# A hybrid diffusion layer: the prompt's output projection and feed-forward moved in between the sample's scan units

## The chip, the cores and the metric

The kernel runs on one core of a Trainium2 chip, as one program. The metric is the device time in microseconds (us), the median of several runs. Engines: PE is TensorE (matrix products), PEld its weight loads, DVE is VectorE, ACT is ScalarE, POOL is GpSimd, SP is SyncE, which issues most transfers here. Every engine works its own queue strictly in order; where two engines depend on each other, one waits at a semaphore.

## The reference

One layer, run for two groups of tokens that share all weights: a prompt of 256 tokens and a sample of 1024 tokens (a grid of 16 rows and 64 columns). The model width is 1024, the feed-forward width 2816, everything is float32. Cut to what matters:

```
h = rmsnorm(x, g_norm1) * (1 + scale_m) + shift_m
proj = h @ w_in
hc, gb, gc, z, xbc, dtf, dtb = split(proj)
out_a = gb * dwconv1d(gc * hc, w_conv_short)
xs, bm, cm = split(silu(dwconv1d(xbc, ...)))
y = ssd_scan(forward) + ssd_scan(backward) + xs * d_skip      # chunks of 128 tokens
y = rmsnorm(y * silu(z), g_ssd_norm)
x = x + gate_m * (concatenate([out_a, y]) @ w_out)
h2 = rmsnorm(x, g_norm2) * (1 + scale_f) + shift_f
u = h2 @ w_up
u = dwconv2d_grid(u) if sample else dwconv1d(u)
ug, uv = split(u)
x = x + gate_f * ((silu(ug) * uv) @ w_down)
y_out = rmsnorm(x, g_final)
```

The modulation vectors (shift, scale, gate) come from a conditioning vector through `w_ada`. The prompt and the sample never mix: the prompt's scan starts from zero, the sample's from given states, and the prompt's final states are outputs.

## The kernel before

Activations lie with channels on the 128 partitions and tokens along the free axis, in eight blocks `k` of 128 channels. A float32 product is made of three: each operand is split in a high part (rounded to the matmul type) and a low part, and `mm3` (line 142) issues, for each `k`, high x high (147), high x low (149) and low x high (151). A weight tile of 1024 x 128 numbers (512 KB) goes through `wload` (line 132): SP loads it into `raw` (line 135), ACT copies it to `whi` (137), and POOL or DVE subtracts to `wlo` (line 73, a helper that records every two-operand operation). `raw` has two buffers, `whi` and `wlo` three each. While the norm pool is open, the prompt's projections pass a buffer of their own to `wload`, from the tag `x` with eight buffers, instead of `raw`.

The stages, by the time at which they lie on the trace: norm statistics, conditioning and first projections (0 to 75 us); the prompt's projections, 24 weight tiles against 256 columns (75 to 162); the sample's scan inputs (162 to 259); the scan (259 to 520); the join of gate, output projection of the first tokens and their norm (520 to 630); the feed-forward (630 to 1618).

The scan has a first pass for both groups and then a second pass of units: 4 for the prompt, 16 for the sample, one unit for each chunk and each of two groups of heads. For a unit, `prep` (lines 559 to 580) loads the decay sums broadcast over partitions into `csb` (562, two buffers), adds a mask on DVE (73), takes eight exponentials on ACT (570) and one of `csb` (572); two units later `output` (line 592) multiplies on PE. `prep` of unit i + 2 is written behind `output` of unit i. Between the units stand *fillers*: the sample's remaining projections, one weight tile against twice 512 columns, 48 matmuls each. `fill` gives one to every second prompt unit and to two of three sample units; what is left runs behind the scan.

Then the gate (lines 695 to 722) multiplies y by silu(z), normalizes and splits it, and the output projection and the feed-forward run in two blocks of tokens: block A, 704 tokens (the prompt's 256 and 448 of the sample), and block B, 576 of the sample. So a weight tile of `w_out` (763) or `w_up` (833) is loaded once for each block and feeds 256 + 448 or 256 + 320 columns, as pairs of matmuls. The feed-forward walks six groups of 4, 4, 4, 4, 3 and 3 channel blocks: up tiles of gate and value, convolution taps on DVE (76, a helper), silu, product and split, and the down projection of the group before (903). A block's edge row for the grid convolution goes through DRAM, as does block B's normalized input.

The order within each engine's queue is set by a scheduler that places the program's instructions by their dependencies and its own estimates.

Of the kernel before, what the change touches and what calls it, by code (L numbers as in the profile page):

```python
# [26 lines left out]
TA = TP + 7 * GW  # L27
TB = TT - TA
OA = TP + 6 * GW
OB = TT - OA  # L30
# [23 lines left out]
def body(nc, tc, A):  # L54
# [6 lines left out]
    def open_pool(name, side="left", **kw):  # L61
        g = tc.tile_pool(name=name, bufs=1, side=side, **kw)
        return g, g.__enter__()
# [50 lines left out]

    g_hs, hsp = open_pool("hsp", side="right")
    g_cv, cv = open_pool("cv", side="right")
    g_xy, xy = open_pool("xy", side="right")
# [24 lines left out]
    def mm3(outs, wh, wl, n):  # L142

        mms = []
        for k in range(n):
            for o, rh, rl in outs:
                nc.tensor.matmul(o, wh[:, k, :], rh(k), start=k == 0, stop=False)  # L147
            for o, rh, rl in outs:
                nc.tensor.matmul(o, wh[:, k, :], rl(k), start=False, stop=False)  # L149
            for o, rh, rl in outs:  # L150
                mm = nc.tensor.matmul(o, wl[:, k, :], rh(k), start=False, stop=k == n - 1)  # L151
# [102 lines left out]
    def ada_block(k):  # L254
        wa = [T(xy, [P, 4, 2 * P], "xs", 4) for _ in range(2)]
        for i in range(2):
            dma(wa[i], A["w_ad1"][k, i])
        pm = psa()
        for j in range(KT):
            q = 32 * (j % 4)  # L260
            nc.tensor.matmul(pm[q:q + 32, 0:2 * P], sc[:, j, :], wa[j // 4][:, j % 4, :],
# [70 lines left out]
    oad = T(dr, [4, 2, P, TT], "oad", 1)  # L332
    zd = T(dr, [4, P, TT], "zd", 1)
# [38 lines left out]
    def zproj(s, j, lo_eng):  # L372
        pp = proj(s, 12 + j, lo_eng)
        z = T(cv, [P, s.T], "xl", 2)
        act(z, pp, AF.Copy)
        nc.scalar.dma_start(zd[j, :, s.t0:s.t0 + s.T], z)
# [105 lines left out]
    def tok_major(s, c, want_raw, r0):  # L482
# [10 lines left out]
        xd = T(sw[0], [P, 512], "xd", 4)  # L493
# [3 lines left out]
        if want_raw:  # L497
            xtok = T(sw[0], [P, 512], "xd", 4)
            act(xtok, xt, AF.Copy)
# [34 lines left out]
    def ssd_pass2(s, fill):  # L534
# [69 lines left out]
        for i in range(2 * s.nc):  # L604
            output(*us[i], fill(s, i))
# [19 lines left out]
    SS.X = [T(xy, [P, TS], "xs", 4) for _ in range(4)]  # L625
# [10 lines left out]
    silu = act(bcall, bcall, AF.Silu)  # L636
    for j in range(4):
# [8 lines left out]
    dts = dtstage(SS, d4_s, silu)  # L646
# [4 lines left out]
    for i in range(N_LOOP, 8):  # L651
# [3 lines left out]
        if i >= 4:  # L655
            ada(i - 2, lambda: T(nrm, [P, 1024], "x", 8))
# [3 lines left out]
    mask = sm[:, wff0:wff0 + 2 * L].rearrange("p (a l) -> p a l", a=2)  # L660
    dma(mask, A["cst"][:, 168:168 + 256].rearrange("p (a l) -> p a l", a=2))
    SP.mask = SS.mask = mask

    def fillers():
        for j in range(4):
            zproj(SS, j, PG)
            yield
        for j in range(4):
            yield from outa(SS, j, PG)

    filler = fillers()

    def fill(s, i):

        if i % 2 == 0 if s.name == "p" else i % 3 != 2:
            next(filler, None)
            return mid_mm[0]
# [442 lines left out]
```

## Time and profile before

| what | us |
| --- | --- |
| median of 3 runs | 1621.23 (1620.62 to 1623.91) |
| the profiled execution's own time | 1629.9 |
| its span | 1628.1 |
| PE busy | 1548.7 |
| DVE busy | 1095.6 |
| ACT busy | 646.3 |
| POOL busy | 519.1 |
| read from / written to device memory | 167.89 MB / 23.67 MB |

Busy times are sums over the span; engines overlap. Matmuls are pipelined, so a matmul's duration on the trace is longer than the spacing of two in a row, and the spacing is what counts for time. PEclk is the share of TensorE's full clock that was granted. In lists of waits each line tells which engine and line waited, for whom, us in total, times, and the longest. A list of one tile gives min/median/max in ns, the first and last start, and the shapes.

### The profile page before, as it was taken

The page shows a single profiled execution, that of the slowest core. Times are in us where ns is not written, and L with a number is a line of the kernel's source. Part 1 is how long each engine was busy: PE and PEld are TensorE (multiplying, and loading weights), DVE is VectorE, ACT ScalarE, POOL GpSimd, SP SyncE. Part 2 cuts the span into 40 slices and gives each one's busy share as a digit, 9 for nine tenths or more (in the row PEclk, how much of TensorE's full clock was granted, in tenths as well). Part 3 has the DMA queues.
Part 4 walks back from the last instruction along what each step waited for, and adds up shares of the span by engine and source line. Part 5 has one row for each costly group of instructions (what it writes and reads, how often), then busy time and mean ns, then how long its engine had stood idle before and what let it go on. Part 6 is the DMA issues. An engine that isn't in the chain of part 4 may idle for free. (4 is left out here: it accounts for less than half of the span.)

```text
span 1628.1 us, 24939 instructions
## 1 busy us (share of the span) xinstructions
PE 1548.7 (95%) x9942; PEld 1411.9 (87%) x9942; DVE 1095.6 (67%) x1637; ACT 646.3 (40%) x1005; POOL 519.1 (32%) x288
## 2 busy tenths in 40 slices
PE   6989999888899799999999999999999999999997
PEld 2688767677777689999999999999999999999996
DVE  5664625445555636698666697656798777887685
ACT  6553534344445424343333353323334232433233
POOL 0445010011111000234434443434455444444442
PEclk8999999999999899999999999999999999999998
DMA  8555275534333551422222243222622223332221
GB/s 295 208 182 162 73 255 191 155 99 78 105 115 128 198 197 53 131 73 86 65 85 79 70 156 115 77 70 70 200 94 92 89 82 98 125 114 73 84 62 65
DMA packets 99534, 193.19 MB, mean 119 GB/s; under 512 B 9274, under 2 KB 51786, under 8 KB 99418
## 3 DMA queue, kind: packets, MB, share of 16 engines
q1 hardware_dynamic: 97690, 188.46, 35.9%
q10 hardware_dynamic: 1728, 3.15, 0.5%
q8 instruction: 78, 1.28, 0.3%
q14 instruction: 38, 0.31, 0.1%
HBM read 167.89 MB, written 23.67 MB: 118 GB/s over the span
## 5 line engine op out<-in xcount | busy, mean ns | idle before, releaser
L76 DVE SCALAR_TENSOR_TENSOR cc<-acc,sm,cc 128x384 f32<-128x384 f32 (+7 forms) x836 | 547.1, 665 | 114.8 <-ACT cc L855 44.9
L73 POOL TENSOR_TENSOR wlo<-raw,whi 128x1024 fp32r<-128x1024 f32 (+2 forms) x115 | 271.6, 2362 | 848.2 <-ACT whi L137 707.7
L137 ACT ACTIVATE whi<-raw 128x1024 fp32r<-128x1024 f32 x126 | 133.1, 1057 | 319.0 <-PE acc L149 279.6
L147 PE MATMUL acc<-ya,whi 128*128 128x256 f32 (+2 forms) x768 | 178.8, 315 | 10.7 <-ACT yb L718 7.7
L149 PE MATMUL acc<-ya,whi 128*128 128x256 f32 (+2 forms) x768 | 178.6, 314 | 0.0
L151 PE MATMUL acc<-ya,wlo 128*128 128x256 f32 (+2 forms) x768 | 177.7, 313 | 0.0
L149 PE MATMUL acc<-oa,whi 128*128 128x256 f32 (+2 forms) x768 | 176.3, 311 | 0.0
L151 PE MATMUL acc<-oa,wlo 128*128 128x256 f32 (+2 forms) x768 | 175.9, 311 | 0.0
L147 PE MATMUL acc<-oa,whi 128*128 128x256 f32 (+2 forms) x768 | 175.8, 311 | 0.0
L76 DVE SCALAR_TENSOR_TENSOR x<-dn,mod,x 128x320 f32<-128x320 f32 (+2 forms) x176 | 96.1, 546 | 91.8 <-PE dn L151 91.1
L147 PEld LDWEIGHTS acc<-ya,whi 128*128 128x128 f32 x768 | 138.8, 191 | 14.0 <-ACT yb L718 8.1
L149 PEld LDWEIGHTS acc<-ya,whi 128*128 128x128 f32 x768 | 139.5, 191 | 3.5 <-issue 0.2
L151 PEld LDWEIGHTS acc<-ya,wlo 128*128 128x128 f32 x768 | 139.1, 191 | 3.4 <-issue 0.2
L151 PEld LDWEIGHTS acc<-oa,wlo 128*128 128x128 f32 x768 | 137.6, 189 | 3.0
L147 PEld LDWEIGHTS acc<-oa,whi 128*128 128x128 f32 x768 | 137.5, 189 | 3.0
L149 PEld LDWEIGHTS acc<-oa,whi 128*128 128x128 f32 x768 | 137.5, 189 | 3.0
L73 POOL TENSOR_TENSOR dlo<-draw,dhi 128x512 fp32r<-128x512 f32 (+1 forms) x88 | 107.7, 1225 | 78.1 <-ACT dhi L912 78.1
L147 PE MATMUL acc<-h,whi 128*128 128x512 f32 x352 | 113.7, 404 | 3.8 <-DVE xs L76 3.8
L149 PE MATMUL acc<-h,whi 128*128 128x512 f32 x352 | 112.7, 399 | 0.0
L151 PE MATMUL acc<-h,wlo 128*128 128x512 f32 x352 | 112.4, 398 | 0.0
L147 PE MATMUL dn<-yb,dhi 128*128 128x320 f32 (+2 forms) x352 | 108.9, 309 | 1.8 <-DVE x L76 1.8
L151 PE MATMUL dn<-yb,dlo 128*128 128x320 f32 (+2 forms) x352 | 108.7, 309 | 0.0
(283 smaller groups left out, 3030.2 us busy)
## 6 DMA issues: line engine op xcount, KB each, us to landing
raw<-in_w_up SPq DMA_DIRECT2D x88, 512.0 KB, 3.5
x<-in_w_ada SPq DMA_DIRECT2D x32, 512.0 KB, 7.4
draw<-in_w_down SPq DMA_DIRECT2D x64, 256.0 KB, 2.8
x<-in_w_in SPq DMA_DIRECT2D x24, 512.0 KB, 4.0
raw<-in_w_in SPq DMA_DIRECT2D x22, 512.0 KB, 4.5
xs<-in_w_ad SPq DMA_DIRECT2D x16, 512.0 KB, 5.1
csb<-csds SPq DMA_DIRECT2D x16, 512.0 KB, 9.1
raw<-in_w_out SPq DMA_DIRECT2D x16, 512.0 KB, 3.6
```

The source lines that it names most:

```text
L73: (eng or V).tensor_tensor(out=out, in0=a, in1=b, op=op)
L76: V.scalar_tensor_tensor(out=out, in0=a, scalar=s, in1=b, op0=op0, op1=op1)
L137: act(hi, raw, AF.Copy)
L147: nc.tensor.matmul(o, wh[:, k, :], rh(k), start=k == 0, stop=False)
L149: nc.tensor.matmul(o, wh[:, k, :], rl(k), start=False, stop=False)
L151: mm = nc.tensor.matmul(o, wl[:, k, :], rh(k), start=False, stop=k == n - 1)
```

## The change

The prompt's tokens are taken out of the two token blocks. The scan is reordered: first both passes of the prompt's scan, with a filler in each of its four units, then the prompt's gate; then the sample's first pass with a filler at every second step; then the sample's 16 units. Units 0 to 7 have one filler each. At unit 8 the pools of the normalized inputs are closed, and a generator `prompt_steps` starts: eight output projection tiles for the prompt's 256 tokens, statistics and second norm, 44 up tiles, 24 down tiles (two blocks of 128 outputs in one `raw` tile) and the final norm. It has 54 steps of one or two weight tiles each; five are taken in each of the last eight units, and the rest behind the scan. All of it goes through `raw`. Each of those units also gates a chunk of 128 tokens (`gate_chunk`) and stores it to DRAM.

The sample's output projection and feed-forward then run in two blocks of 512 tokens, one matmul of 512 columns for each product; the feed-forward's second block starts 64 tokens earlier for the grid's edge row, so that the down projection has 448 and 576 tokens. The second block's normalized input stays on chip. z gets its silu when it is projected, and SP instead of ACT stores it. Four conditioning loads move: two into the prompt's projections, two within the sample's. The output projection runs its k in the order 4 to 7, 0 to 3. Counted over the program: 8736 products before and 7488 now, with the same columns; weight loads of `w_up` rise from 88 to 132, of `w_out` from 16 to 24, and 56 half tiles of `w_down` are added; POOL instructions rise from 284 to 372, DVE's from 1628 to 1685.

```diff
...
-    def mm3(outs, wh, wl, n):
+    def mm3(outs, wh, wl, ks):
 
         mms = []
-        for k in range(n):
+        ks = list(range(ks)) if isinstance(ks, int) else ks
+        for k in ks:
             for o, rh, rl in outs:
-                nc.tensor.matmul(o, wh[:, k, :], rh(k), start=k == 0, stop=False)
+                nc.tensor.matmul(o, wh[:, k, :], rh(k), start=k == ks[0], stop=False)
             for o, rh, rl in outs:
                 nc.tensor.matmul(o, wh[:, k, :], rl(k), start=False, stop=False)
             for o, rh, rl in outs:
-                mm = nc.tensor.matmul(o, wl[:, k, :], rh(k), start=False, stop=k == n - 1)
+                mm = nc.tensor.matmul(o, wl[:, k, :], rh(k), start=False, stop=k == ks[-1])
...
-        act(z, pp, AF.Copy)
-        nc.scalar.dma_start(zd[j, :, s.t0:s.t0 + s.T], z)
+        s.zact = act(z, pp, AF.Silu)
+        dma(zd[j, :, s.t0:s.t0 + s.T], z)
...
+        if j in (1, 3):
+            ada_s(2 + j // 2)
...
-            ada(i - 2, lambda: T(nrm, [P, 1024], "x", 8))
+        if i in (3, 5):
+            ada_s(4 + i // 5)
...
+    for step in ssd_pass1(SP):
+        step()
+    ssd_pass2(SP, lambda i: project())
...
+    steps = ssd_pass1(SS)
+    for i, step in enumerate(steps):
+        step()
+        if i % 2 == 1:
+            project()
+        if i == 1:
+            gate_p()
+
+
+    ph = Norm()
+
+    def open_prompt():
+        close_pool(g_hs)
+        close_pool(g_cv)
+        ph.g_mx, ph.mx = open_pool("mx", side="right")
+        ph.g_pf, ph.pf = open_pool("pf", side="right")
...
+    def prompt_steps():
+        pf = ph.pf
+        mix = load_mix(ph.mx, 0, TP)
+        x1 = [T(pf, [P, 4, TP], "x1p", 2) for _ in range(2)]
+        for q in range(2):
+            dma(x1[q], xT[:, 4 * q:4 * q + 4, 0:TP])
+        xv = [x1[m // 4][:, m % 4] for m in range(KT)]
...
+        for m in range(KT):
+            if m % 2 == 0:
+                pps = pair_psum()
+            wh, wl = split_wout(m)
+            pp = pps[m % 2]
+            last_mm.append(mm3([(pp, lambda k: mix[k][0], lambda k: mix[k][1])], wh, wl, KS)[-1])
+            stt(xv[m], pp, col(2, m, 0), xv[m], ALU.mult, ALU.add)
             yield
...
+        def up(m, pp, out, lo_eng):
+            wh, wl = wload(A["w_up"][m], lo_eng)
+            last_mm.append(mm3([(pp, lambda k: h2[k][:, 0], lambda k: h2[k][:, 1])], wh, wl, KT)[-1])
+            w = [smv("wff")[:, m * 9 + t:m * 9 + t + 1] for t in range(9)]
+            act(out, pp, AF.Identity, scale=w[4], bias=smv("bff")[:, m:m + 1])
...
+        def down(gi, g, m):
+            nj = GROUPS[gi]
+            j0 = sum(GROUPS[:gi])
+            raw = T(wst, [P, KT, P], "raw", 2)
+            for i in range(2):
+                off = (j0 * KT + (m + i) * nj) * P * P
+                dma(raw[:, i * nj:(i + 1) * nj],
+                    A["w_down"][off:off + nj * P * P].rearrange("(p j c) -> p j c", p=P, j=nj))
+            wh = T(wst, [P, KT, P], "whi", 3, F32R)
+            act(wh[:, 0:2 * nj], raw[:, 0:2 * nj], AF.Copy)
+            wl = T(wst, [P, KT, P], "wlo", 3, F32R)
+            tt(wl[:, 0:2 * nj], raw[:, 0:2 * nj], wh[:, 0:2 * nj].bitcast(F32), ALU.subtract, PG)
+            pps = pair_psum()
+            for i in range(2):
+                mm = mm3([(pps[i], lambda k: g[0][:, k], lambda k: g[1][:, k])],
+                         wh[:, i * nj:(i + 1) * nj], wl[:, i * nj:(i + 1) * nj], nj)
+                last_mm.append(mm[-1])
+                stt(xv[m + i], pps[i], col(5, m + i, 0), xv[m + i], ALU.mult, ALU.add)
...
+            for i in range(nj):
+                pps = pair_psum()
+                up(j0 + i, pps[0], cg[:, i], PG)
+                up(N_FF + j0 + i, pps[1], cu[:, i], PV if i % 2 else PG)
+                yield
+                if prev is not None:
+                    down(gi - 1, prev, 2 * i)
+                    if i == nj - 1 and nj < 4:
+                        down(gi - 1, prev, 6)
+                    yield
...
+        for m in range(0, KT, 2):
+            down(len(GROUPS) - 1, prev, m)
+            yield
...
+    def gate_chunk(c):
...
+        hi = T(pf, [P, 4, L], "gh", 1, F32R)
+        act(hi, uf, AF.Copy)
+        tt(u, uf, hi.bitcast(F32), ALU.subtract)
+        for i, src in enumerate((hi, u)):
+            dma(yd[:, i, :, tl].rearrange("j p t -> p j t"), src.bitcast(F32))
...
-    def fill(s, i):
-
-        if i % 2 == 0 if s.name == "p" else i % 3 != 2:
-            next(filler, None)
-            return mid_mm[0]
...
+    N_PROJ = 8
+    more = [None]
+
+    def fill_s(i):
+        if i < N_PROJ:
+            return project()
+        if i == N_PROJ:
+            for _ in filler:
+                pass
+            open_prompt()
+            more[0] = prompt_steps()
+        else:
+            gate_chunk(i - N_PROJ - 1)
+        for _ in range(N_FILL):
+            next(more[0], None)
         return last_mm[-1]
 
-    for step in ssd_pass1(SS) + ssd_pass1(SP):
-        step()
-    ssd_pass2(SP, fill)
-    ssd_pass2(SS, fill)
-    for _ in filler:
-        pass
+    N_FILL = 5
+    ssd_pass2(SS, fill_s)
+    gate_chunk(7)
...
+    for _ in more[0]:
+        pass
...
+    def wout(mix, a):
         for m in range(KT):
+            wh, wl = split_wout(m)
+            pp = pac()
+            mm3([(pp, lambda k: mix[k][0], lambda k: mix[k][1])], wh, wl, KS)
+            xx = x1[m][:, a:a + HB]
+            stt(xx, pp, col(2, m, 1), xx, ALU.mult, ALU.add)
...
+    h2 = [[], []]
+    wout(mix1, 0)
+    for f in norm2_steps(0, ph.mx, h2[0]):
         f()
+    wout(mix2, HB)
+
...
+    NOS = [O1, O2]
+    TOS = [0, O1]
...
-    DPARTS = [[(0, TP, 0), (TP, NO, 1)], [(0, 320, 1), (320, NO, 1)]]
+    DPARTS = [[(0, O1)], [(0, 320), (320, O2)]]
...
```

On PE, in one of the sample's later units before: what stands around the unit's output (`yp`; `acc` with `h`, `whi`, `wlo` is a filler):

```order
L147 MATMUL acc_552_3259<-h_55_228,whi_550_3255 128x512 x2
L505 MATMUL sa_545_3231<-xd_542_3224,btok_541_3222 128x256 x2
L149 MATMUL acc_552_3259<-h_56_231,whi_550_3255 128x512 x2
L151 MATMUL acc_552_3259<-h_55_228,wlo_551_3257 128x512
L147 MATMUL acc_552_3259<-h_67_277,whi_550_3255 128x512 x2
```

and in one of the last eight units now (`mx` is the prompt's normalized input, `sa<-gz` the norm of a gated chunk):

```order
L595 MATMUL yp_723_4686<-wm_635_4063,xd_630_4050 64x128
L595 MATMUL yp_723_4686<-csb_634_4061,sfw_585_3724 64x128
L595 MATMUL yp_723_4686<-csb_634_4061,sb_625_4036 64x128
L881 MATMUL sa_737_4749<-gz_735_4742,ones_4_70 128x128 x2
L149 MATMUL acc_740_4764<-mx_656_4208,whi_742_4767 128x256
L151 MATMUL acc_740_4764<-mx_656_4208,whi_742_4767 128x256
L153 MATMUL acc_740_4764<-mx_656_4208,wlo_743_4769 128x256
```

A filler's matmuls came in twos of 512 columns for each weight block; now each weight block has a single matmul of 256 columns.

On ACT, between two filler weight copies (`whi`) in the scan before:

```order
L570 ACTIVATE wm_504_2888<-wm_504_2888,toks_289_1717 128x128 x8
L572 ACTIVATE csb_503_2886<-csb_503_2886 128x1024
L137 ACTIVATE whi_550_3255<-raw_549_3253 128x1024
L384 ACTIVATE cv_509_2957<-acc_508_2908 128x1024
L570 ACTIVATE wm_511_2975<-wm_511_2975,toks_289_1717 128x128 x8
L572 ACTIVATE csb_510_2973<-csb_510_2973 128x1024
L137 ACTIVATE whi_569_3398<-raw_568_3396 128x1024
```

and in one of the last eight units now (line 138 is the copy in `wload`, 824 that of the down tiles, 811 the copy of an up result, 573 and 575 the exponentials, 885 to 890 the gated chunk):

```order
L824 ACTIVATE whi_748_4834<-raw_747_4831 128x1024
L885 ACTIVATE gr_738_4752<-sa_737_4749,epsc_5_72 128x128
L886 ACTIVATE gr_738_4752<-gr_738_4752 128x128
L890 ACTIVATE gh_739_4759<-gu_736_4744 128x512
L138 ACTIVATE whi_753_4868<-raw_752_4866 128x1024
L811 ACTIVATE cg_710_4583<-acc_740_4764,sm_1_63 128x256
L573 ACTIVATE wm_734_4728<-wm_734_4728,toks_322_1864 128x128 x8
L575 ACTIVATE csb_733_4726<-csb_733_4726 128x1024
L138 ACTIVATE whi_756_4901<-raw_755_4899 128x1024
L811 ACTIVATE cu_711_4584<-acc_740_4764,sm_1_63 128x256
L824 ACTIVATE whi_759_4935<-raw_758_4932 128x1024
```

Before, one weight copy stood between the exponentials of two units; now about seven do, and the exponentials stand between two neighbouring copies.

On SP, the loads and stores of the same stretch now (`yd` is the gated chunk's store, `gz` a chunk of z):

```order
L821 DMA raw_747_4831<-in_w_down 128x512 x2
L136 DMA raw_752_4866<-in_w_up 128x1024
L565 DMA csb_733_4726<-csds_118_569 128x8x128
L136 DMA raw_755_4899<-in_w_up 128x1024
L893 DMA yd_121_572<-gh_739_4759 128x4x128
L893 DMA yd_121_572<-gu_736_4744 128x4x128
L872 DMA gz_816_5380<-zd_122_573 128x4x128
L821 DMA raw_758_4932<-in_w_down 128x512 x2
L136 DMA raw_763_4967<-in_w_up 128x1024
```

The weight loads share the queue with the unit's `csb` and with the chunk's two stores and its load, which stand between them.

413 lines of the change are left out of this document (218 added, 195 removed).

## The prediction

> **What bounds the kernel now.** I read the page's span and shares first, then the table of time windows by stage.
>
> ```profile
> span 1628.1 us, 24939 instructions
> PE 1548.7 (95%) x9942; PEld 1411.9 (87%) x9942; DVE 1095.6 (67%) x1637; ACT 646.3 (40%) x1005; POOL 519.1 (32%) x288
> ...
> core 0: us, PE busy (x) PEld busy (x) DVE busy (x) ACT busy (x) POOL busy (x), PEclk, DMA share, GB/s
> ...
> 75.00:162.00 87.00, 79.21 (x604) 75.42 (x603) 50.62 (x67) 44.74 (x65) 45.05 (x19) 0.94 0.56 184
> ...
> 259.00:520.00 261.00, 233.51 (x1342) 187.47 (x1341) 145.35 (x196) 112.60 (x248) 35.53 (x13) 0.97 0.40 113
> 520.00:630.00 110.00, 97.95 (x526) 87.58 (x525) 54.60 (x68) 43.23 (x54) 0.00 (x0) 0.92 0.49 176
> 630.00:1618.00 988.00, 983.15 (x6709) 963.32 (x6707) 756.19 (x1177) 363.62 (x536) 412.13 (x237) 1.00 0.29 92
> ```
>
> TensorE is busy 95% of the span. In the feed-forward (630 to 1618) it hardly pauses and its clock is full, so only fewer or shorter matmuls can save there. In the scan (259 to 520) it idles 261 - 233.5 = 27.5 us. At the join of gate and output projection (520 to 630) it idles 12 us, and a clock of 0.92 costs another 98 x 0.08 = 8. The prompt projections (75 to 162) show TensorE near its limit with tiles 256 columns wide and **eight** weight buffers. The waits say why the feed-forward is safe:
>
> ```profile
> POOL wlo L73 <- ACT whi L137: 743.7, 104, 154.6
> ACT whi L137 <- PE acc L149: 295.1, 94, 15.0
> ```
>
> There ScalarE's weight copy (line 137) waits for TensorE to free a buffer: the weights come sooner than they are used. What the change asks is whether that still holds where each weight tile feeds 256 columns instead of 704 or 576.
>
> **a) Fewer matmuls.** The output projection and the up projection took, for each k and each of the three products, pairs of 256 + 448 and 256 + 320 columns. Now it is one of 256 and two of 512. Columns are equal; 52 weight tiles x 24 products = 1248 matmuls go away. The timeline of TensorE gives the spacing:
>
> ```profile
> 899.73 0.28 PE L147 MATMUL dn<-g,dhi 128*128 128x256 f32 x1
> ...
> 900.81 0.34 PE L147 MATMUL dn<-g,dhi 128*128 128x384 f32 x1
> ...
> 902.90 0.48 PE L147 MATMUL acc<-ya,whi 128*128 128x256 f32 x2
> ...
> 903.86 0.48 PE L147 MATMUL acc<-ya,whi 128*128 128x256 f32 x2
> ```
> ```profile
> 1304.38 0.43 PE L147 MATMUL acc<-ya,whi 128*128 128x256 f32 x2
> ...
> 1305.98 0.43 PE L147 MATMUL acc<-ya,whi 128*128 128x256 f32 x2
> ```
> ```profile
> 414.53 0.62 PE L147 MATMUL acc<-h,whi 128*128 128x512 f32 x2
> ...
> 420.94 0.62 PE L151 MATMUL acc<-h,wlo 128*128 128x512 f32 x2
> ```
>
> Nine of 256 columns take 1.08 us, 0.120 each; twelve of 384 take 2.09 (to 902.90), 0.174 each. The pair 256 + 448 takes 0.96/3 = 0.320, the pair 256 + 320 takes 1.60/6 = 0.267. Twenty-eight of 512 take 6.41, 0.229 each. Before: 0.320 + 0.267 = 0.587. After: 0.120 + 2 x 0.229 = 0.578. 1248 x 0.009 = **-11.2 us**. A fixed cost per matmul, from 256 and 384 columns (0.120 - 256 x 0.054/128 = 0.012 to 0.013), would give -16: the other bound. The down projection keeps 2112 matmuls and its columns: nothing.
>
> The Trainium skill ("TensorE: Matmul & The Clock Gate", "Wait — 56ns, not 53.3ns?") puts a warm stream at N/2.4 GHz plus about 2.5 ns for each matmul; by it 1248 fewer would be worth about 3 us, an estimate. Here 256 columns took 120 ns, where that formula has 109, so the trace shows more cost per matmul, and the trace decides.
>
> **b) The join.** Before, gate, statistics and bulk loads stood between the last scan unit and the output projection: 20 us lost in 520 to 630, as above. Now the gate runs chunk by chunk in the units, and 14 of the prompt's 54 steps lie between the scan and the sample's output projection. They cover the last chunk's way through DRAM. I leave 5 us of loss: **-15** (bounds 0 and -20).
>
> **c) The scan's idle time.** Before, 13 of 20 units had a filler of 48 matmuls of 512 columns. Now the prompt's four and the sample's first eight all have one, and the last eight have the prompt block. I take half of the 27.5 us: **-14** (bounds 0 and -27).
>
> **d) The prompt block.** It decides the sign. Its 8 + 44 + 24 = 76 weight tiles, all 256 wide, are read once more than before, and they go through `raw` with **two** buffers, not through the eight of the prompt projections. TensorE needs 24 x 0.120 = 2.88 us for a tile, 1776 matmuls or 213 us in all. The eight units have their own matmuls:
>
> ```profile
> 421.50 0.43 PE L592 MATMUL yp<-wm,xd 128*64 128x128 f32 x2
> ...
> 423.86 0.71 PE L147 MATMUL acc<-h,whi 128*128 128x512 f32 x2
> 424.41 0.40 PE L149 MATMUL acc<-h,whi 128*128 128x512 f32 x1
> 424.64 0.42 PE L552 MATMUL sa<-bc,bc 128*128 128x128 f32 x2
> 426.10 0.43 PE L592 MATMUL yp<-wm,xd 128*64 128x128 f32 x2 [1.03 <-DVE xs L76]
> ...
> 428.83 0.58 PE L149 MATMUL acc<-h,whi 128*128 128x512 f32 x1
> ```
>
> From 421.50 to 428.83 two units ran; less the filler's 0.78 and the idle 1.03, 5.5 us, 2.8 a unit. With 8 x 2.8 = 22 the block is 235 us of TensorE.
>
> Now the chain that makes one weight tile. It shows only at the start of the output projection, where TensorE waits for it (SyncE's queue, ScalarE and VectorE on the timeline), and in the lists of single tiles:
>
> ```profile
> 592.55 6.30 SPq L135 DMA_DIRECT2D raw<-in_w_out  x3
> ...
> 596.18 1.06 ACT L137 ACTIVATE whi<-raw 128x1024 fp32r<-128x1024 f32 x1 [3.97 <-DMA raw<-in_w_out]
> ...
> 597.27 1.22 DVE L73 TENSOR_TENSOR wlo<-raw,whi 128x1024 fp32r<-128x1024 f32 x1 [3.61 <-ACT whi L137]
> ```
> ```profile
> L73 POOL TENSOR_TENSOR wlo<-raw,whi x20: 2402/2407/2413, 701.1 to 889.2; 128x1024 fp32r<-128x1024 f32 x20
> ...
> DMA to landing us min/median/max: 3.3/3.4/4.2
> ```
> ```profile
> L73 POOL TENSOR_TENSOR wlo<-raw,whi x12: 2352/2830/2927, 311.4 to 508.0; 128x1024 fp32r<-128x1024 f32 x12
> ...
> DMA to landing us min/median/max: 4.8/7.0/8.8
> ```
>
> A buffer is free again when its low part is subtracted: 596.18 - 592.55 = 3.63 to the copy, 1.06 copy, then 1.22 on VectorE or 2.41 on GpSimd: 5.97 or 7.15 us. Over two buffers that is 2.99 or 3.58 us a tile, and 66 of the 76 go to GpSimd: 66 x 3.58 + 10 x 2.99 = 266 us, **31 more** than TensorE's 235. During the scan GpSimd took 2.83 (VectorE's work beside it): 0.42/2 for the 47 such tiles inside the units, **+10**.
>
> Then ScalarE's order. In six units eight exponentials and one more (lines 570, 572) stand between two weight copies, and wait for a `csb` load:
>
> ```profile
> ACT wm L570 <- DVE wm L73: 105.0, 17, 10.2
> ...
> DVE wm L73 <- DMA csb<-csds: 56.7, 15, 7.2
> ```
> ```profile
> L570 ACT ACTIVATE wm<-wm,toks 128x128 f32<-128x128 f32 x128 | 39.2, 389 | 94.8 <-DVE wm L73 94.8
> ...
> L572 ACT ACTIVATE csb<-csb 128x1024 f32<-128x1024 f32 x20 | 20.9, 1043 | 0.0
> ```
> ```profile
> L73 DVE TENSOR_TENSOR wm<-csb,sm x18: 1216/1226/1228, 300.9 to 502.2; 128x1024 f32<-128x1024 f32 x18
> ...
> DMA to landing us min/median/max: 8.0/9.1/10.4
> ```
>
> ScalarE already waited here 6 us at a time; then nothing urgent stood behind it. Now the next weight copy does: from the issue of `csb` 9.1 + 1.2 + 8 x 0.39 + 1.04 = 14.5 us, while its tile has landed after 3.4 to 7. It is 7 to 11 late, of which a ready tile or two (2.9 each) hides 3 or so: 6 us in each of six units, **+36** (bounds 0 and 66). After such a stop the clock is low:
>
> ```profile
> 551.50:555.00 3.50, 0.00 (x0) 0.00 (x0) 3.50 (x5) 1.08 (x2) 0.00 (x0) 0.50 0.67 250
> 555.00:562.50 7.50, 7.33 (x32) 6.92 (x33) 3.50 (x5) 1.11 (x2) 0.00 (x0) 0.67 0.75 269
> ```
>
> 7.5 x 0.33 = 2.5 us; for four of the six stops **+10**. The prompt's norm has nothing of the block beside it, less the tiles already prefetched: **+5**. Sum of d: 31 + 10 + 36 + 10 + 5 = **+92**. The bounds are +10 (the norm and a few misses, all else hidden) and +140 (each `raw` at the scan's median landing of 7.0 would add (7.0 - 3.4)/2 = 1.8 for some 27 tiles near bulk loads). SyncE's order adds to this: stores of gated chunks stand ahead of weight loads, and wait for GpSimd and VectorE.
>
> **e) The rest.** Two of the conditioning blocks now lie in the prompt projections, which have 7.8 us of idle but a DMA share of 0.56: +3. In the sample's feed-forward VectorE must keep up in blocks of 512:
>
> ```profile
> L76 DVE SCALAR_TENSOR_TENSOR cc<-acc,sm,cc 128x441 f32<-128x441 f32 x176 | 118.7, 675 | 4.5
> ...
> L76 DVE SCALAR_TENSOR_TENSOR cc<-acc,sm,cc 128x504 f32<-128x504 f32 x88 | 64.7, 735 | 0.6
> ```
>
> Four taps of 504, two of 441 and two of 448 (0.68) are 5.65 us a tile, 11.3 a pair; with the product, the down sums and the norm steps some 15.0, against 48 x 0.229 + 24 x 0.200 = 15.8 of TensorE. That is tight: +5. Together **+8** (0 to +30).
>
> **The sum**, on the profiled execution's 1629.9 us: 1629.9 - 11.2 - 15 - 14 + 92 + 8 = 1689.7. The median of the runs, 1621.23, is 8.7 lower; so 1681, and I say **1680**. All gains together are 40 us: the change breaks even where d is +32, a pace of (235 + 32)/76 = 3.51 us a tile, just under what two buffers and GpSimd give without any disturbance.
>
> **Rivals.** *The chain keeps up* (0.27): TensorE paces the block at 235/76 = 3.1 us, d is +10, and the time is 1680 - 82 = **1598**, faster. For it: `csb` is asked for two units ahead, and the waits of ScalarE before cost TensorE little; three buffers of copies smooth a stop. Against it: the 3.58 above. It decides below 3.51 us a tile. *A clean chain of two buffers, nothing blocked by the exponentials* (0.13): d is 31 + 10, **1629**, from 1612 to 1645. For it: the waits above end before TensorE's next weights in the old scan. Against it: ScalarE's queue is strict. *The block is hidden, and VectorE becomes the bound in the sample's feed-forward* (0.05): 10% on its 15.0 exceeds 15.8 by 0.7 less the slack of other pairs, 0.5 x 44 = 22: **1620**. Against it: 756 of 988 us busy before. Forecast, slower: 0.55, by itself 1645 to 1725.
>
> **How the numbers follow.** About 0.2% is what a measurement of this kernel can tell from no change, 3.2 us. Faster: the first rival, and a small part of the second and third, 0.32. Same: parts of the second and third, 0.06. Slower: 0.62. The range takes in most of the first rival and the forecast's upper bound: 1590 to 1725.
>
> **What would show it.** Right: in the last eight units TensorE is below 90% busy, weight copies stand 3.5 us or more apart, SyncE's weight loads wait for GpSimd's subtraction, and copies wait behind the exponentials with a lowered clock behind them; the gap ahead of the sample's output projection is short; matmuls of 512 columns are 0.229 apart. Wrong: copies 3.1 us apart in the block with TensorE near 95%, or a feed-forward in which TensorE waits for VectorE.

## The result and the profile after

| | before | after |
| --- | --- | --- |
| median, us | 1621.19 | 1780.69 (1771.31 to 1784.96) |
| ratio after / before | | 1.0972, 95% interval 1.0923 to 1.1022 |
| span of the profiled execution, us | 1628.1 | 1782.2 |
| forecast, us | | 1680 (1590 to 1725) |

The change makes the kernel 9.7% slower: 159 us, where +59 was forecast. The page of the kernel after, for comparison with the first rows of the prediction:

```profile
span 1782.2 us, 23202 instructions
## 1 busy us (share of the span) xinstructions
PE 1583.9 (89%) x8726; PEld 1342.7 (75%) x8726; DVE 1137.2 (64%) x1694; ACT 755.7 (42%) x1127; POOL 713.0 (40%) x376
...
PE   6978999999966767667669999999999999999997
...
PEclk9998999999977889879889999999999999999999
```

One stretch stands out, slices 12 to 21: TensorE's digits fall to 6 and 7, its clock to 7 to 9. The table of time windows, cut at its edges:

```profile
core 0: us, PE busy (x) PEld busy (x) DVE busy (x) ACT busy (x) POOL busy (x), PEclk, DMA share, GB/s
260.00:508.00 248.00, 237.01 (x1228) 191.02 (x1227) 115.22 (x142) 95.41 (x171) 42.77 (x17) 0.99 0.36 109
508.00:937.00 429.00, 290.64 (x2070) 270.66 (x2068) 184.71 (x307) 182.61 (x265) 172.05 (x73) 0.84 0.48 156
937.00:1045.00 108.00, 105.77 (x451) 86.25 (x451) 70.08 (x72) 42.45 (x55) 47.09 (x20) 0.97 0.30 103
1045.00:1770.00 725.00, 720.38 (x3636) 625.28 (x3635) 624.39 (x968) 293.37 (x444) 382.28 (x229) 1.00 0.31 102
```
```profile
937.00:1782.00 845.00, 829.38 (x4099) 713.35 (x4098) 700.95 (x1049) 338.60 (x504) 433.06 (x252) 0.99 0.31 103
```

508 to 937 is the last eight scan units and the prompt block: from the last projection's end to the sample's first output product. It takes 429 us for 235 us of TensorE's work (213 for the block, 22 for the units): 138 us idle, and 291 x 0.16 = 46 at the lowered clock. On either side the change gains. Before, the first output product came at 555; now it is 508 plus the units' 22: 25 us gained. From there to the end it was 1073, of which 213 for the prompt; now 845: 15 gained. The stretch itself loses 429 - 235 = 194, and 194 - 25 - 15 = 154 is the difference of the spans.

Who waits for whom within the stretch:

```profile
DVE x1p L77 <- PE acc L153: 95.2, 32, 11.9
...
PE acc L149 <- DVE x1p L77: 43.4, 28, 7.7
...
ACT wm L573 <- DVE wm L74: 41.1, 7, 8.6
DVE wm L74 <- DMA csb<-csds: 36.4, 7, 7.7
```
```profile
SPq L136 <- POOL wlo L74: 131.5, 39, 9.4
```

And one of the six stops, on the chain of waits:

```profile
635.75 1.74 PE yp L595 x24
...
637.50 9.66 DMA csb<-csds
...
647.19 1.23 DVE wm L74
648.42 0.39 DVE cg L77
648.81 0.40 DVE x1p L77
...
649.26 0.58 PE acc L149
```

A unit's products free a `csb` buffer, the next load goes out at once and takes 9.66 us. VectorE has the mask addition at the head of its queue and waits for it; behind it stands the sum of the first half of a down pair (`x1p`), and TensorE's second half waits for that sum. TensorE idled 7 us here. The forecast had this load, but put ScalarE's weight copy behind it; VectorE's sums stand there too.

### The profile page after: what moved, and what is told of

Its sections match the earlier page's. It is cut to its first block, busy times and chain, and to the rows that moved or that the text cites. A ratio compares the mean times of both kernels' runs of the same rounds, so it can differ in the third digit from the quotient of the medians.

```text
span 1782.2 us, 23202 instructions
## 1 busy us (share of the span) xinstructions
PE 1583.9 (89%) x8726; PEld 1342.7 (75%) x8726; DVE 1137.2 (64%) x1694; ACT 755.7 (42%) x1127; POOL 713.0 (40%) x376
## 4 chain that ended last, share of the span: by engine, by line
PE 67%; DMA 9%; DVE 9%; issue 5%; POOL 4%; ACT 4%; SPq 1%; DVEq 0%; ACTq 0%; POOLq 0%
PE acc L149 16%; PE acc L153 16%; PE acc L151 16%; DMA csb<-csds 4%; PE dn L153 4%; PE dn L151 4%; PE dn L149 4%; POOL wlo L74 3%; DVE cc L77 2%; PE acc L312 1%; DMA raw<-in_w_down 1%; PE yp L595 1%; ACT whi L138 1%; PE sa L508 1%; DVE wm L74 1%
## 5 line engine op out<-in xcount | busy, mean ns | idle before, releaser
L74 POOL TENSOR_TENSOR wlo<-raw,whi 128x1024 fp32r<-128x1024 f32 (+2 forms) x197 | 465.7, 2367 | 859.9 <-ACT whi L138 704.8
L77 DVE SCALAR_TENSOR_TENSOR cc<-acc,sm,cc 128x504 f32<-128x504 f32 (+2 forms) x748 | 497.6, 686 | 83.1 <-ACT cc L1018 35.6
L149 PE MATMUL acc<-mx,whi 128*128 128x512 f32 (+1 forms) x1248 | 457.8, 368 | 39.4 <-DVE x1p L77 14.9
L151 PE MATMUL acc<-mx,whi 128*128 128x512 f32 (+1 forms) x1248 | 454.1, 364 | 0.6 <-DVE mx L74 0.5
L153 PE MATMUL acc<-mx,wlo 128*128 128x512 f32 (+1 forms) x1248 | 452.2, 363 | 0.2 <-DVE wlo L74 0.2
L149 PEld LDWEIGHTS acc<-mx,whi 128*128 128x128 f32 x1248 | 247.5, 199 | 76.7 <-issue 16.6
L151 PEld LDWEIGHTS acc<-mx,whi 128*128 128x128 f32 x1248 | 247.4, 198 | 33.6 <-DVE mx L74 1.5
L153 PEld LDWEIGHTS acc<-mx,wlo 128*128 128x128 f32 x1248 | 246.3, 197 | 35.1 <-DVE wlo L74 0.4
L151 PE MATMUL dn<-g,dhi 128*128 128x320 f32 (+2 forms) x480 | 154.6, 322 | 2.4 <-POOL g L74 2.4
L149 PE MATMUL dn<-g,dhi 128*128 128x320 f32 (+2 forms) x480 | 154.2, 322 | 1.5 <-ACT g L1039 1.5
L153 PE MATMUL dn<-g,dlo 128*128 128x320 f32 (+2 forms) x480 | 154.5, 322 | 0.7 <-POOL dlo L74 0.7
L151 PEld LDWEIGHTS dn<-g,dhi 128*128 128x128 f32 x480 | 90.7, 189 | 7.9 <-POOL g L74 3.3
L149 PEld LDWEIGHTS dn<-g,dhi 128*128 128x128 f32 x480 | 90.7, 189 | 7.0 <-ACT g L1039 2.1
L153 PEld LDWEIGHTS dn<-g,dlo 128*128 128x128 f32 x480 | 90.8, 189 | 4.1 <-POOL dlo L74 1.5
```

The lines of the kernel that those rows point to most:

```text
L74: (eng or V).tensor_tensor(out=out, in0=a, in1=b, op=op)
L77: V.scalar_tensor_tensor(out=out, in0=a, scalar=s, in1=b, op0=op0, op1=op1)
L149: nc.tensor.matmul(o, wh[:, k, :], rh(k), start=k == ks[0], stop=False)
```

## Experiments

The rivals when the experiments began: stops behind the `csb` load, a chain of two weight buffers, the sums between two halves, and the block's own order. All ratios below are against the kernel before, on the same chip. The kernel after by itself ranged over 14 us in four runs, and the experiments have two to four runs (`split512` ten), so a gain of a few us in a median is not told apart from none. For the larger steps there is a second measure at the end of "The block by itself": the stretch from the end of the last filler to the sample's first output product.

### One suspect at a time, in the change's order

`late`: the mask addition and the exponentials of a unit are put behind the third prompt step of the next unit.

```diff
...
-        for _ in range(N_FILL):
+        for k in range(N_FILL):
             next(more[0], None)
+            if k == 2 and late:
+                late.pop()(last_mm[-1])
...
```

> From the eleventh sample unit on, the mask addition on VectorE and the nine exponentials on ScalarE of the unit after next are put behind the third prompt step of the next unit, so that their load of decay sums has about 10 us to land before an in-order queue reaches them. The changed kernel's six stops after that load cost 47 us of idle TensorE and some 20 of lowered clock. If the load standing at the head of VectorE's and ScalarE's queues makes the stops, the time falls by 40 to 65 us, to 1715 to 1740, and VectorE's wait for the load in the block goes from 36 us to under 10. If the two weight buffers set the pace, or the sums that the second half of a pair waits for, it stays within 15 us of 1781.

1777.9 us (1.0946): 3 us less, within the spread of the kernel after. The edit did what it was meant to do: VectorE's wait for `csb` in the stretch fell from 36.4 to 8.2 us. But the wait changed its place, and ScalarE now waits for weights.

```profile
ACT whi L138 <- DMA raw<-in_w_up: 49.1, 15, 6.4
```

In the kernel after, that wait was 17.1 us. The order of the queues is not the cause alone. That the load itself keeps others back is the next suspect; `whole_a` below tries it.

`halves`: both products of a pair ahead of both sums.

```diff
...
                 last_mm.append(mm[-1])
+            for i in range(2):
                 stt(xv[m + i], pps[i], col(5, m + i, 0), xv[m + i], ALU.mult, ALU.add)
```

> In the prompt block both products of a pair of outputs (output and down projection) are written ahead of the two sums, so TensorE's second half no longer waits for VectorE's sum of the first. The changed kernel has 28 such waits, 43 us together, of which some 24 us fall in the stops behind the decay sums. If this wait is a cause by itself, the time falls by 15 to 35 us, to 1746 to 1766. If it only passes on a VectorE that is late for other reasons, the next pair waits instead and less than 10 us are gained.

1770.5 us (1.0901): 10 us, a median just below the fastest run of the kernel after (1771.3). `raw4`: every second weight tile of the block from two more buffers (the norm's temporary has one buffer instead of two, for room).

```diff
...
+    def praw():
+        rc[0] += 1
+        return T(ph.pf, [P, KT, P], "rp", 2) if rc[0] % 2 else T(wst, [P, KT, P], "raw", 2)
...
-            raw = T(wst, [P, KT, P], "raw", 2)
+            raw = praw()
...
```

> The prompt block's weight tiles get four buffers instead of two (every second one from a pool of its own). If the chain of load, copy and subtraction over two buffers sets the pace (my sum had 31 us for it), the time falls by 30 to 50 us, to 1730 to 1750, and SyncE's waits for GpSimd's subtraction in the block, 197 us now, fall below 100. If the stops behind the decay sums set it, the loads come earlier but the copies stay behind the exponentials: 0 to 15 us gained.

1775.1 us (1.0929): 6 us, again within the spread. Weights now came sooner (ScalarE's waits for them in the stretch fell from 43 to 10 us), but nothing clear was gained: the two buffers of my sum set nothing here by themselves. `all3` has the three edits.

> The three edits together: decay sums' work behind the third step, both halves of a pair ahead of their sums, four weight buffers. Singly they gave 3, 10 and 6 us. If they are small separate losses, together 15 to 25 us: 1756 to 1766. If the limits stand one behind another, so that taking one away only shows the next (with the late additions ScalarE's waits for weight loads rose from 17 to 49 us), together they give much more than their sum: 1700 to 1740.

1761.2 us (1.0840): 19 us, clear of the spread and about the plain sum.

### The block behind the scan

`behind`: in the program's order no step stands between the units; the forty stand behind them.

```diff
-    N_FILL = 5
+    N_FILL = 0
...
     gate_chunk(7)
+    for _ in range(40):
+        next(more[0])
```

> No prompt step lies between the last eight scan units; the 40 steps run right behind the scan. So the block runs without scan units beside it, at the price of units with nothing to cover their latency. If two buffers alone set the block's pace, copies stand 3.4 to 3.6 us apart, 76 tiles take 260 to 275 us and the norm 15; eight bare units take some 15 us each by the load's 10 us and the exponentials, less where two overlap: 80 to 120. Sum 355 to 410 against 429 now, so 1710 to 1765. If the block is slow by itself (sums, loads of 256 columns), its tiles stay 5 us apart and the time rises to 1830 or more.

1760.3 us (1.0838): 20 us **faster** than with the block between the units. The eight units now take from 501 to 599, and from there to the sample's first output product it is 314 us, 308 of them the block.

The units are not bare on the trace, though. The scheduler still placed 159 of the block's products among them, 6.6 weight tiles or 19 us, and the gate's chunks stand there too. So 22 + 19 = 41 us of products take 98, and the remaining 194 take 308. Both stretches are slow, and the second has no unit's load beside it. The chain of waits in the first:

```profile
502.94 9.22 DMA csb<-csds
...
535.24 10.62 DMA csb<-csds
...
549.87 9.46 DMA raw<-in_w_out
...
573.21 8.95 DMA csb<-csds
```

Three loads of decay sums make 29 of its 98 us, a weight load that waits beside them 9.5. The gate's chunks are on this chain as well (`sa` of line 881, the logarithm of line 885), and no run takes them out while leaving the rest as it is.

`behind3` adds `halves` and `raw4`, `spread3` also spreads the 16 sample projections over the units as in the kernel before.

> The prompt block behind the scan, with four weight buffers and both halves ahead of the sums. With two buffers its 76 tiles took 308 us, where TensorE's matmuls alone are 213. If buffers and sums set that pace, the block comes down to 240 to 260 and the time to 1695 to 1715. If something else does (the chain silu, product, split ahead of each group's down projection, or GpSimd's 2.4 us a tile), it stays above 285 us and the time above 1735.

> As the run with the block behind the scan, four buffers and both halves first, but the 16 sample projections spread over prompt and sample units (2 and 14) instead of the first twelve places, so that no row of bare units is left; the gate's chunks lie between the block's steps. Eight bare units took 76 us, 54 more than their matmuls. If the price of the scan is the units without a filler, this gives 30 to 45 us over the run before it: 1655 to 1675. If units cost their latency with fillers too, 0 to 10.

1766.5 us (1.0873) and 1753.1 us (1.0790). Neither buffers nor sums set the block's pace. (Two of the expectations give 76 us for eight bare units; on the trace of `behind` it is the 98 above, with 6.6 tiles among them.) In `spread3` the scan ended 55 us sooner, but 41 of it came back: the gate's chunks and loads then lay in the block.

### The load of the decay sums

`whole_a` and `whole_b` change one layout, in the kernel after and before. In DRAM a unit's eight rows of 128 lie together, so a load reads one piece of 4 KB for each partition and not eight of 512 bytes that lie 4 KB apart.

```diff
-        s.csd = T(dr, [2, 2, 4, n], f"csd{name}", 1)
+        s.csd = T(dr, [2, n // L, 2, 4, L], f"csd{name}", 1)
...
-            dma(csb, s.csd[g].rearrange("a h l -> (a h) l")[:, u.cl].unsqueeze(0)
-                .broadcast_to([P, 8, L]))
+            dma(csb.rearrange("p a l -> p (a l)"),
+                s.csd[g, u.c].rearrange("a h l -> (a h l)").unsqueeze(0).broadcast_to([P, 8 * L]))
```

> The decay sums of a unit are laid out in DRAM as one piece of 4 KB instead of eight rows of 512 bytes; the units' loads read the same 512 KB in longer pieces. In the changed kernel such a load takes 9.7 us to land, a weight load beside it 8.6 us against 3.2 alone. If this load is what the block's stops and the bare units wait for, it lands in 3 to 5 us and the time falls by 35 to 60 us, to 1720 to 1745. If the load's length does not matter (late additions gave 3 us), it stays above 1770; the landing does not change if the pieces' length is not what makes it slow.

> The same edit in the kernel before: one piece of 4 KB. There a filler of 11 us covers the load in 13 of 20 units and TensorE idles 27 us in the scan. If the load's latency makes part of that, 3 to 12 us are gained, 1609 to 1618; if the fillers hide it, within 2 us of before.

The lists of the tile `csb`, of the kernel after and then of `whole_a`:

```profile
L565 SPq DMA_DIRECT2D csb<-csds x16: 370/371/386, 311.4 to 764.3; - x16
...
DMA to landing us min/median/max: 3.8/9.1/10.2
```
```profile
L568 SPq DMA_DIRECT2D csb<-csds x16: 319/320/442, 307.0 to 719.9; - x16
...
DMA to landing us min/median/max: 4.0/4.3/4.6
```

(The 3.8 in the first list is a load of the prompt, which the list's last line also counts; the sample's alone are 8.6 to 10.2.)

`whole_a` takes 1731.5 us (1.0656), 49 us less. Not all of it lies in the block: the last filler ends at 488 instead of 508, and the stretch from there to the sample's first output product takes 397 instead of 430. So 32 us of the loss in the block are this load, and the rest was gained before it.

The edit changes two things, the length of the pieces and their distance in DRAM. The kernel after has the length without the distance: the prompt's loads also read eight pieces of 512 bytes for each partition, but its 256 tokens put them 1 KB apart and not 4 KB. Their list:

```profile
L565 SPq DMA_DIRECT2D csb<-csdp x2: 371/371/371, 284.9 to 299.1; - x2
...
DMA to landing us min/median/max: 3.8/3.8/3.9
```

They land as soon as pieces of 4 KB do: in `whole_a`, where the prompt's loads are one piece too, the same load takes 3.9. So the length of 512 bytes by itself did not make the sample's loads slow. The distance between the rows is the difference that is left in view; no run changes it alone.

`whole_b` takes **1592.3 us, 0.9804 (0.9787 to 0.9821)**: 2% faster than the kernel before, almost three times the most that was expected. Its first output product comes at 518 instead of 555 (5 of these 37 us lie ahead of the scan, where the profiled execution of the kernel before was slow). What had looked like 27 us of mixed idle time in the scan and part of the 12 at the join was mostly this load:

```profile
259.00:487.00 228.00, 224.12 (x1330) 181.69 (x1330) 143.56 (x190) 115.74 (x250) 31.32 (x13) 0.99 0.38 128
```
```profile
DVE wm L73 <- DMA csb<-csds: 10.0, 9, 2.2
```

The wait was 56.7 us before.

`whole4` is `whole_a` with four buffers, halves first, and each group's down projection one pair of up tiles later:

> The changed kernel's order with the one-piece load, four weight buffers, halves ahead of sums and the later down projection. If the losses are separate ones, the gains add: 20 of the three small edits, 35 to 60 of the load, 10 to 25 of the later down: 1680 to 1715. If the block is bound by weight loads beside the scan's other transfers, 1735 or more.

1723.2 us (1.0605): 8 us more. What was eased here still stood behind other limits, as the next section shows.

### The block by itself

`behind4` has the later down projection and accumulators of its own for it, with two weight buffers; `behind5` adds four; `behind6` moves the low parts of the second up tile, the down tiles and the split from GpSimd to VectorE.

```diff
-            pps = pair_psum()
+            pps = [psa()[:, 0:TP] for _ in range(2)]
...
+            ms = [0, 2, 4, 6]
...
-                if prev is not None:
-                    down(gi - 1, prev, 2 * i)
...
+                if prev is not None and i > 0:
+                    todo = (1, 1, 2)[i - 1] if nj == 4 else 2
+                    for _ in range(todo):
+                        down(gi - 1, prev, ms.pop(0))
```

> The block behind the scan with two weight buffers, and two edits of its own order: the down projection of a group starts one pair of up tiles later (so silu, product and split have 4 tiles of TensorE's work to hide behind instead of 2), and its results get accumulators of their own instead of taking turns with the up tiles in two. In the block's clean stretch a group of 12 tiles takes 50 us, 34.6 of matmuls; 5.4 us of the idle time stand at the split, 4.5 at the accumulators. If those make the block's own loss, a group comes down to 40 us and the time from 1760 to 1705 to 1725. If two weight buffers do after all (3.58 a tile, 43 a group), 1730 to 1740.

> The block behind the scan with the later down projection, accumulators of its own, and four weight buffers: the three limits of its clean stretch at once. Each alone or in pairs left a tile at 4.1 to 4.2 us (50 us for 12), where two buffers and GpSimd give 3.58 and TensorE 2.88. If they are limits side by side, of which each hides the others, a tile now takes 3.0 to 3.4 us and the time falls from 1760 to 1690 to 1715. If GpSimd's queue or the granted clock is the limit, a tile stays near 4 us and the time above 1740.

> As the run before it, with the low parts of the second up tile of a pair, of the down tiles and of the split on VectorE (1.2 us) instead of GpSimd (2.4 us). If GpSimd's queue is what is left, this gives 15 to 35 us more, 1665 to 1695. If TensorE's own pace and the clock are left, less than 8.

They took 1755.4 (1.0803), 1727.6 (1.0654) and 1710.9 us (1.0551). A group of 12 tiles (288 products, 34.6 us) in `behind`, and the like in `behind5` and `behind6`:

```profile
765.00:816.00 51.00, 38.44 (x288) 36.26 (x288) 16.36 (x27) 20.89 (x25) 26.98 (x12) 0.93 0.38 124
```
```profile
759.00:798.00 39.00, 35.34 (x292) 34.71 (x293) 16.60 (x28) 20.81 (x24) 28.13 (x13) 1.00 0.51 166
```
```profile
754.00:791.00 37.00, 33.93 (x288) 33.22 (x288) 24.45 (x35) 21.12 (x25) 10.43 (x5) 1.00 0.55 171
```

51, 39 and 37 us: 4.2, 3.2 and 3.1 a tile, and the clock comes back to 1.00. Two buffers, accumulators, the wait at the split and GpSimd's queue were limits side by side. The buffers taken away without the rest (`behind3`) gave nothing, the split and the accumulators together (`behind4`) little, all three (`behind5`) much; GpSimd's queue was only tried on top. The wait at the split, in `behind`'s chain of waits:

```profile
709.83 3.34 POOL wlo L74
713.17 2.32 POOL gp L74
...
715.53 0.58 PE acc L151
```

The split's low part (`gp`) stands behind a weight's low part on GpSimd, and the first down product that reads it stands behind both.

Last, all the easing with the one-piece load, between the units (`whole6`) and behind them (`behind7`):

> The changed kernel's own order, between the scan units, with the one-piece load and the block's limits eased as far as that order lets them be: four weight buffers, later down, halves ahead of sums, low parts shared between VectorE and GpSimd. The step before it (low parts on GpSimd) took 1723. Behind the scan the shared subtraction gave 17 us. If VectorE has room beside the scan units, 1700 to 1712; if its queue, which also carries the units' additions, is late, 1720 or more.

> The block behind the scan with all four limits eased (1711) and the one-piece load. Eight bare units took some 76 us at 9.7 us a load; at 4.3 us they should be held by ScalarE's exponentials and VectorE, some 5 to 6 us each: 30 to 38 us less, 1673 to 1681. Then the order of the change, block between units, hides nothing that a block behind them does not. If the units stay at 9 us, 1705.

1696.8 us (1.0452) and 1678.0 us (1.0336). Between the units the same work is still 19 us slower (the easing differs too: `whole6` shares the accumulators and puts the halves first, `behind7` has accumulators of its own). `behind7` fell in its range partly by luck: the expectation puts 30 to 38 us on the bare units, but they went from 98 to 82, 16 us; about 20 came in the scan before them.

The stretch from the last filler's end to the sample's first output product, in one profiled execution each. TensorE's own work in it is 235 us, and the forecast had 235 + 92 = 327:

| run | us | run | us |
| --- | --- | --- | --- |
| after | 430 | `behind` | 412 |
| `late` | 422 | `behind3` | 414 |
| `raw4` | 424 | `behind4` | 400 |
| `halves` | 410 | `behind5` | 377 |
| `whole_a` | 397 | `behind6` | 357 |
| `whole6` | 361 | `behind7` | 341 |

### The blocks of 512 alone

`split512` is the kernel before with the prompt and 512 sample tokens in block A and 512 in block B (gate's z and the norm's temporary with one buffer, for room).

```diff
-TA = TP + 7 * GW
+TA = TP + 8 * GW
...
-    PARTS_B = [(256, 0, 256, 1), (512, 256, TB, 1)]
+    PARTS_B = [(512, 0, TB, 1)]
```

> The kernel before with one part of the change alone: the prompt's 256 tokens stay with the sample's first 512 in block A, block B is 512, each as one matmul of 512 columns beside the prompt's 256. For room the gate's z and the norm's temporary have one buffer instead of two. My term a gives 11 us for the matmuls that go away (16 by the other bound, 3 by the formula I set against it); the single buffers may cost 0 to 8. So 1605 to 1622. If VectorE becomes the bound in the feed-forward (14 taps of up to 504 columns beside the prompt's), 1635 or more.

1623.9 us, 0.9992 (0.9982 to 1.0002): no change. From the first output product to the end it takes 1063.6 us, 9.3 less than before; that product comes 5.9 later (561.1 for 555.2), at the gate, although the scan's first load had gone out 5.5 sooner. VectorE kept up.

> The kernel before with the one-piece load and the blocks of 512 (the prompt in block A): the two parts that helped or did no harm. The first gave 32.8 us, the second 0.6 in all (9 us less from the first output product to the end, lost again at the join to the single buffers). If they add, 1585 to 1593.

1592.9 us, 0.9826 (0.9803 to 0.9849): the two do not add beyond the one-piece load. Here too the later stretch is 8 us shorter and the product comes 8 us later.

## Why the prediction was right or wrong

- **What bounds the kernel.** Half right. The feed-forward was TensorE's, and the prompt block did decide the sign. But the scan's idle time was read as something that fillers close, without asking what it waits for. Fillers did close part of it (11 us idle from 260 to 508 in the kernel after), and the load held more. The row with the waits for `csb`, 56.7 us, was in the prediction and used for ScalarE alone. `whole_b` shows what was in it: 33 us.
- **a, fewer matmuls, -11.** Right: 9.3 in `split512`, and 8 between `whole_b` and `whole512`. The fixed cost per matmul that 256 and 384 columns show was the poorer bound. The formula of the Trainium skill ("TensorE: Matmul & The Clock Gate", "Wait — 56ns, not 53.3ns?"), 3 us, was too small. Matmuls of 512 columns are 0.229 apart in the kernel after, as forecast.
- **b and c, join and scan, -15 and -14; e, +8.** Their sum was -21; the stretches outside the block show -40, of which a is 9: -31. The sign and the place are right. The part of e for VectorE did not come: in the feed-forward TensorE is busy 720 of 725 us. What the two conditioning loads cost was not measured alone.
- **d, the prompt block, +92. This step failed:** it measured +194. The sum took one chain of two buffers as the block's pace by itself, 31 us, and laid a few disturbances by the units on top. `behind` shows that the block loses most of it with no unit beside it: 194 us of products take 314 to the next stage, 120 lost, at 4.2 us a tile in its even stretch where the forecast chain gives 3.6. Another 57 were lost in the window of the last eight units. Term by term:
  - *Two buffers, 31.* Wrong as a mechanism that acts by itself: four buffers gave nothing clear in the change's order. Behind the scan, once accumulators and the split were out of the way, they counted for 23 to 28 us (from `behind4` to `behind5`, by the stretch and by the medians; the two differ in the buffers and the norm's temporary): near the size of the term, but masked in the kernel as it is. A chain worked out from one stage's durations is a bound, not a sum, where other waits run at the same pace. (The chain's own terms add up to 5.91 and 7.10 us, not 5.97 and 7.15; that is 2 us on the term.)
  - *GpSimd beside VectorE, 10.* In the kernel after, its weight subtraction took 2.38 in the median in the block, not 2.83. But its queue mattered: with part of it on VectorE 17 to 26 us were gained.
  - *Stops behind the exponentials, 36 and clock 10.* Right in kind and place: the stops are there, started by a load of 9.6 to 10.2 us. `whole_a` puts a price of 32 us on the load in this stretch, where 46 were forecast. The engine was only half right: VectorE's sums and TensorE's second halves stood behind it as well, and freeing the queues alone (`late`) gave nothing clear.
  - *Norm, 5.* Too small, but not measured alone. In `behind6` the first 73 us behind the last unit hold three output tiles, the norm and nine up tiles, 35 us of products, at a clock of 0.77 and 241 GB/s of loads.
  - *Put at nothing:* that each group's down projection starts two tiles behind its silu and shares accumulators with the up tiles, which leaves TensorE waiting at the split; and the latency of the last units, where the block does not cover it. In `behind` their window takes 98 us for 41 of products, 82 for 36 with the short load (`behind7`). The load and the gate's chunks stand on its chain; only the load was tried.
- **The rival of the hidden block** (1598) fell with this, and so did the clean chain of two buffers (1629): `behind` has no `csb` load beside the even stretch of the block and it still ran at 4.2 us a tile. The third rival, VectorE as the bound of the sample's feed-forward (1620), did not come either: TensorE is busy there.
- **The signs** named for "right" nearly all came, which shows how little they tell of the size: TensorE is busy 68% of the stretch, SyncE's weight loads wait for GpSimd (131.5 us), the clock is down to 0.84. The gap ahead of the sample's output projection is not short: TensorE idles 7.6 us there.
- **The range** ended at 1725. Its upper bound took d as +140; the terms were each bounded, but what was not on the list was not.

What stays open: `behind7`, with everything eased that was found, is still 55 us above the kernel before on its chip and 86 above `whole_b`. By their windows, its last eight units lose 46 us (82 for 36 of products) and the block behind them 61 (260 for 199); why was not tried further.

## What to carry to other kernels

Before moving work into idle time, find what the idle time waits for: here a load of eight short rows that lay 4 KB apart, and laying it out in one piece gave 2% in an edit of a few lines where the large restructuring lost 10%. Look also at what the filling work needs: the old filler was 11 us of matmuls on two short conversions, the new one needs a copy, a subtraction and a sum every 3 us. Work that waits behind a slow load on an engine's queue is a sign, not yet a price: `late` took the wait out of the queue, and the time stayed, with the weights late instead. Moving a step in the program does not yet move it on the chip: check on the trace where the scheduler put it. A pace worked out for one limit says little where several lie close together; ease them together before you call one of them harmless.

## What the runs showed of the hardware that was not expected

The same 512 KB to 128 partitions landed in 9.1 us (median of 11 in the kernel after) as eight rows of 512 bytes, 4 KB apart in DRAM, and in 3.8 to 5.1 us (15 landings in six runs) as one piece of 4 KB. While the first ran in the block, six weight loads of 512 KB that were issued beside it landed in 7.3 to 10.2 us, where the others took 3.2 in the median.

Eight rows of 512 bytes that lay 1 KB apart landed in 3.8 and 3.9 us in the kernel after, and in 3.6 to 5.4 in the other eleven changed kernels that kept those rows; in the kernel before, where two ran at once, in 5.7 and 6.2. Other traffic is not the difference either: beside one weight load, the transfers ran at some 90 GB/s in a load of the sample (476.6 to 485.6 us) and at some 340 in one of the prompt (284.8 to 288.9). The Trainium skill ("DMA: Bandwidth & Descriptors", "Specifications") gives 512 B as the smallest transfer at line rate. The trace agrees in that the prompt's loads, in pieces of this length, landed no later than those of 4 KB. What makes the sample's load slow stays open; the distance of its rows is what differs.
